# A two-layer hybrid DiT kernel: block 0's rows loaded among the first modulation tiles, and residual-row stores tied to program order

## The chip, the core and the metric

The kernel runs on one core of a Trainium2 chip. The metric is the device time of one execution in microseconds (us). Five engines work side by side: TensorE (PE, matrix multiplies), VectorE (DVE), ScalarE (ACT), GpSimd (POOL) and SyncE (SP). In this kernel SP issues every transfer between HBM and the on-chip memory, in order, on one hardware queue. Each engine works through its own list of instructions in order; when the instruction at its head waits, all that stands behind it on that engine waits too.

## The reference

Two layers, each with a mixer and a feed-forward part, on 1024 latent tokens and 256 context tokens of width 1024:

```python
h = x + _pos_embed_2d(rows, D)[None]
hc = ctx
for l in range(DEPTH):
    mod_x = (silu(c) @ w_mod[l] + b_mod[l])[:, None, :]
    sh1, sc1, gt1, sh2, sc2, gt2 = split(mod_x, 6)      # and mc for the context from c_ctx
    ux = _modulate(h, norm1_g[l], sh1, sc1) @ w_in[l]   # rmsnorm(h) * (1 + scale) + shift
    uc = _modulate(hc, norm1_g[l], mc[0], mc[1]) @ w_in[l]
    # four column groups of u: bidirectional RWKV-7, pooling, 2-D Fourier, gated convolution
    h = h + gt1 * _mix_and_project(ux, y_rwkv_x, ...)
    h = h + gt2 * _swiglu(_modulate(h, norm2_g[l], sh2, sc2), ffn_w_in[l], ffn_w_out[l])
    # the same for hc, except in the last layer
return _rmsnorm(h, final_norm_g)
```

## The kernel before, in words

The width of 1024 is held as NK = 8 rows of 128 partitions. The tokens are three blocks: block 0 and block 1 with 512 latent tokens each, block 2 with the 256 context tokens. A tile of the residual stream is `h[k][tb]`, row k of block tb, 128 x 512 or 128 x 256 floats. A matrix product is made of three TensorE products, since weights and activations are each split into a high part (ACT, `split`, L324) and a low part (L325).

**Order of the work.** The program is traced as straight code with Python generators that are woven into one another. A list scheduler then sets the order of the instructions of each engine, from priorities that follow the order of tracing and from a timeline of its own. What it chooses is fixed in the program; at run time every engine follows its list. `s.pin(...)` (L164, `keep_in_program_order`) takes an instruction out of that choice: it is issued behind the instruction of the same engine that was traced just before it.

**The start (`run`, L1256 to L1293).** The modulation vectors of layer 0 come first: scale (j = 1) and shift (j = 0), two halves each, four generators in the list `mods`. Each has eight tiles of `in_wmod` of 256 KB (`mod_tile`, L216). Two generators use TensorE (`mod_pe`), one DVE (`mod_sum` with `dve`, L261 and L263), one ACT and POOL (`mod_sum` without it, L266, L269 and L267). Then `load(0, k)` loads the eight rows of block 0 (L1266) and adds the position rows on DVE (L1275). The sums of squares of block 0 (`norm_r`, `rstd_g`: ACT squares, TensorE sums into `ps`, ACT root, DVE reciprocal L354, TensorE spread into `ps`) give the norm; `norm_g` (L388, L389, L390) writes the normed activations, and `first_tb` multiplies them by the first columns of `in_win` into `pf`. Blocks 1 and 2 follow.

**The projections of a layer.** `start()` (L1309 to L1316) loads the Fourier tiles `swA` and `swB` and stores all rows `h[k][tb]` to HBM as `hd`, because the residual is needed again only at the output projection: 24 stores in layer 0 (16 of 256 KB, 8 of 128 KB), 16 in layer 1. In layer 0 it is called after the first columns have been shifted (`shift`, L400 to L405; one Tanh part, L784) and stored as `rw` (`spill`, L446). Beside it runs `conv1`: each of its column blocks is multiplied into a `pc` bank of PSUM, of which there are two, and ACT copies the bank out (`dense_tb`, L427). Its results go to HBM (`hc`, L446) and come back as shifted windows (`window`, L506) for the 31-tap convolution on DVE, ACT and POOL (L522 to L535). Meanwhile a second set of modulation tiles for layer 0 (`mod_step`) comes through L216 and is taken by ACT (L269 for the first tile, L266 after it) and POOL (L267), and by TensorE.

The loop of TensorE products of one row block (`dense_tb`) and the loop of the stores are short:

```python
s.mm(ps[:, :n], wh, ah, i == 0, False)
s.mm(ps[:, :n], wh, al, False, False)
s.mm(ps[:, :n], wl, ah, False, i == NK - 1)
```

Of the kernel before, what the change touches and what calls it, by code (L numbers as in the profile page):

```python
# [19 lines left out]
NK = 8  # L20
# [72 lines left out]
class _Kernel:  # L93
# [1162 lines left out]
    def run(s, nlayers):  # L1256
        nc = s.nc
        s.consts()

        h = s.rows(NK, ("x", "c"))  # L1260
# [17 lines left out]
        for k in range(NK):  # L1278
            for g in mods:
                next(g)  # L1280
        for k in range(NK):
            load(0, k)
        s.lab("norm1")
        r = [s.norm_r(h, 0, sq="c2")]
# [15 lines left out]
        for l in range(nlayers):  # L1300
# [6 lines left out]
            hd = [s.dr.tile([128, 1280], F32, name=s.nm("hd")) for _ in range(NK)]  # L1307

            def start(h=h):  # L1309
                for i in range(2):  # L1310
                    nc.sync.dma_start(swA[i], s.I["swA"][l][:, i * 512:(i + 1) * 512])
                    nc.sync.dma_start(swB[i], s.I["swB"][l][:, i * 512:(i + 1) * 512])
                for tb in tbs:
                    for k in range(NK):
                        n = TBS[tb][2]
                        nc.sync.dma_start(hd[k][:, 512 * tb:512 * tb + n], h[k][tb])  # L1316

            hid = [s.dr.tile([128, 1280], F32, name=s.nm("hid")) for _ in range(NFF)]
            h2, acts2 = [[None] * 3 for _ in range(NK)], [[None] * 3 for _ in range(NK)]
# [44 lines left out]
            s.weave = _Weave(s, None)  # L1364
            s.weave.start(side())
            s.rwkv1(l, R, first, acts, ("x", "c") if not last else ("x",), segs, swA, ymix, start)
            s.rwkv2(R, fill())
            h, acts = h2, acts2
# [35 lines left out]
            for k in range(NK):  # L1404
                for tb in tbs:
                    n = TBS[tb][2]
# [6 lines left out]
            for f0, f1 in FF2:  # L1413
                s.lab("ffn2")
                hr = [s.act_row(segs) for f in range(f0, f1)]
                for f in range(f0, f1):
                    for tb in tbs:
                        n = TBS[tb][2]
# [291 lines left out]
class _Weave:  # L1710
# [5 lines left out]
    def next(s, g, end):  # L1716
        s.k.lab(s.labs.get(g, s.k.label))
        r = next(g, end)
        s.labs[g] = s.k.label
        if r is end and g in s.tails:  # L1720
            s.tails.remove(g)
        return r
# [169 lines left out]
```

## Time and profile before

| | us |
|---|---|
| median of 3 runs | 3349.17 |
| the three runs | 3340.93, 3349.17, 3352.15 |
| profiled execution | 3351.38 |
| its span, first to last instruction | 3349.6 |

| engine | busy us | share of the span |
|---|---|---|
| PE | 3000.7 | 90% |
| DVE | 2109.8 | 63% |
| POOL | 1385.8 | 41% |
| ACT | 1257.5 | 38% |

The span is 1.8 us shorter than the profiled execution's own time, and that execution is 2.2 us above the median of the runs. A row of an engine's timeline gives the start in us, the duration, the engine, the source line with the operation, what is written from what is read (buffer numbers left out), shapes, a count where several follow each other, and in brackets the idle time before it and what ended it. In a row for several instructions the duration runs from the start of the first to the end of the last. SPq rows are issues of transfers, not the transfers themselves. A table by windows gives for each stretch the busy time and count of PE, PE's weight loads, DVE, ACT and POOL, then the granted TensorE clock as a share of full speed, the busy share of the DMA engines, and GB/s.

### The profile page before, as it was taken

To read this page: it belongs to the slowest core of one execution; us is meant where nothing else is said; L and a number is where in the kernel's file an instruction comes from. 1 tells how busy PE (TensorE), PEld (TensorE's weight loads), DVE (VectorE), ACT (ScalarE), POOL (GpSimd) and SP (SyncE) were. 2 spreads that over 40 slices of the span, in tenths; PEclk is the share of its full clock that TensorE was granted. 3 is DMA by queue.
4 is the path that set the end of the run, shared out by engine and by line. 5 is a ranking of instruction groups with operands and counts; after the bars stand their busy time and mean duration, and the time that the engine had idled before them with its cause. 6 is when DMAs were issued, how large, how long until landed. Compare 5 with 4: busy or idle time off the path is not lost.

```text
span 3349.6 us, 52386 instructions
## 1 busy us (share of the span) xinstructions
PE 3000.7 (90%) x18888; PEld 2410.5 (72%) x18888; DVE 2109.8 (63%) x3498; ACT 1257.5 (38%) x2575; POOL 1385.8 (41%) x1484
## 2 busy tenths in 40 slices
PE   6989997877889999999999978988877799999998
PEld 3657765766678888888888766756665588888787
DVE  6679666666374988644545598666665755554535
ACT  4446433443363222223212455333443433333212
POOL 2366224563168554435310064245550454545400
PEclk8989887787899999999999988987787799999999
DMA  7422344465455444337412212345553322224312
GB/s 265 165 92 97 102 117 136 124 174 156 144 190 164 149 132 151 125 98 233 139 35 78 87 53 90 117 134 139 156 159 88 128 92 79 82 89 164 123 39 78
DMA packets 375818, 415.48 MB, mean 124 GB/s; under 512 B 115587, under 2 KB 214916, under 8 KB 375558
## 3 DMA queue, kind: packets, MB, share of 16 engines
q1 hardware_dynamic: 375558, 412.13, 39.4%
q8 instruction: 149, 2.44, 0.3%
q14 instruction: 111, 0.91, 0.1%
HBM read 306.49 MB, written 100.27 MB: 121 GB/s over the span
## 4 chain that ended last, share of the span: by engine, by line
PE 55%; DVE 14%; DMA 9%; issue 3%; SPq 1%; ACT 1%; POOL 1%; DVEq 0%; POOLq 0%; ACTq 0%
PE pc L153 17%; PE ps L153 17%; PE pb L153 14%; PE pf L153 8%; DMA t<-Ad 3%; DVE c L532 2%; DMA Td<-t 1%; DVE t L1050 1%; DVE t L947 1%; DVE t L1043 1%; DVE f L325 1%; DVE t L956 1%; DVE t L1469 1%; DMA t<-ho 1%; DVE t L1493 1%
## 5 line engine op out<-in xcount | busy, mean ns | idle before, releaser
L153 PE MATMUL pc<-t,f 128*128 128x512 f32 (+1 forms) x3108 | 754.4, 392 | 41.3 <-ACT t L427 16.0
L153 PEld LDWEIGHTS pc<-t,f 128*128 128x128 f32 x3108 | 581.6, 195 | 182.9 <-ACT t L427 20.5
L153 PE MATMUL ps<-t,f 128*128 128x512 f32 (+1 forms) x2094 | 517.0, 393 | 18.4 <-ACT t L324 7.7
L153 PE MATMUL pb<-t,f 128*128 128x512 f32 (+1 forms) x2094 | 470.5, 370 | 8.4 <-ACT t L1468 4.9
L153 PEld LDWEIGHTS ps<-t,f 128*128 128x128 f32 x2094 | 390.8, 190 | 99.8 <-ACT t L324 8.2
L153 PEld LDWEIGHTS pb<-t,f 128*128 128x128 f32 x2094 | 370.4, 190 | 78.8 <-ACT t L1468 6.0
L1515 ACT CAST f<-c 128x512 fp32r<-128x512 f32 x316 | 196.0, 621 | 536.7 <-PE ps L153 132.0
L1517 POOL TENSOR_TENSOR f<-c,f 128x512 fp32r<-128x512 f32 x135 | 186.5, 1381 | 426.2 <-ACT f L1515 411.7
L153 PE MATMUL pf<-t,f 128*128 128x512 f32 (+2 forms) x1500 | 314.2, 364 | 14.2 <-DVE t L1044 4.0
L324 ACT CAST f<-m 128x512 fp32r<-128x512 f32 (+1 forms) x236 | 134.7, 576 | 436.3 <-PE pb L153 226.4
L153 PEld LDWEIGHTS pf<-t,f 128*128 128x128 f32 (+1 forms) x1500 | 249.5, 198 | 61.4 <-ACT f L324 4.4
L530 POOL TENSOR_TENSOR c<-c,cp 128x352 f32<-128x352 f32 (+2 forms) x168 | 183.3, 1092 | 145.9 <-ACT c L523 71.3
L1517 DVE TENSOR_TENSOR f<-c,f 128x512 fp32r<-128x512 f32 x181 | 158.6, 878 | 134.8 <-ACT f L1515 134.4
L153 PE MATMUL pf<-c,f 128*128 128x512 f32 (+1 forms) x704 | 200.5, 416 | 30.0 <-DVE t L1684 20.3
L325 POOL TENSOR_TENSOR t<-c,t 128x512 fp32r<-128x512 f32 (+1 forms) x110 | 135.1, 1266 | 173.8 <-PE ps L153 99.5
L153 PE MATMUL ps<-t,t 64*128 64x128 f32 (+2 forms) x1032 | 159.9, 341 | 38.9 <-DVE t L956 23.4
L532 DVE SCALAR_TENSOR_TENSOR c<-c,dv,c 128x352 f32<-128x352 f32 (+2 forms) x238 | 190.5, 829 | 2.0
L153 PEld LDWEIGHTS ps<-t,t 64*128 64x128 f32 (+1 forms) x1032 | 133.6, 231 | 60.4 <-issue 20.4
L153 PEld LDWEIGHTS pc<-t,t 128*64 128x64 f32 (+2 forms) x2484 | 124.6, 161 | 71.8 <-issue 28.6
L153 PE MATMUL pc<-t,t 128*64 128x64 f32 (+3 forms) x2484 | 156.2, 258 | 20.9 <-DMA t<-t 11.8
L153 PEld LDWEIGHTS pf<-c,f 128*128 128x128 f32 x704 | 131.5, 214 | 60.1 <-issue 19.1
L261 DVE SCALAR_TENSOR_TENSOR cp<-m,sc,cp 128x512 f32<-128x512 f32 x140 | 137.5, 1003 | 43.0 <-DMA m<-in_wmod 42.3
(256 smaller groups left out, 4731.3 us busy)
## 6 DMA issues: line engine op xcount, KB each, us to landing
c<-in_ffin SPq DMA_DIRECT2D x176, 256.0 KB
m<-in_wmod SPq DMA_DIRECT2D x116, 256.0 KB
t<-rw SPq DMA_DIRECT2D x232, 128.0 KB
hid<-t SPq DMA_DIRECT2D x88, 256.0 KB
c<-hid SPq DMA_DIRECT2D x88, 256.0 KB
m<-in_ffout SPq DMA_DIRECT2D x80, 256.0 KB
t<-in_wmod SPq DMA_DIRECT2D x76, 256.0 KB
m<-in_win SPq DMA_DIRECT2D x64, 256.0 KB
```

What stands on the lines that cost most here:

```text
L153: s.nc.tensor.matmul(o, l, r, start=start, stop=stop)
L261: nc.vector.scalar_tensor_tensor(acc[t], w, sc, acc[t], ALU.mult, ALU.add)
L324: r = s.nc.scalar.copy(hi, src)
L325: (eng or s.lo_eng).tensor_tensor(lo, src, hi.bitcast(F32), ALU.subtract)
L530: nc.gpsimd.tensor_tensor(g, g, t_, ALU.add)
L532: nc.vector.scalar_tensor_tensor(a, w[:, j:j + m], tap(j), a, ALU.mult, ALU.add)
L947: nc.vector.scalar_tensor_tensor(KRv[:, :, p, 0, 1:64], k2[:, :, p, 1:64], -2.0, P2[:, :, p, 0:63], ALU.mult, ALU.mult)
L956: nc.vector.tensor_tensor(BKv[rows, :, :, 1 - h, :], cv(kd)[rows], cv(iP)[rows], ALU.mult)
L1043: nc.vector.tensor_tensor(tv, at(x, o, [0, m], [1, 4], [32, 4]), at(T_, r0, [32, m], [0, 4], [1, 4]), ALU.mult)
L1050: nc.vector.tensor_tensor(tv, at(x, o + 4, [0, m], [1, n], [32, 4]), at(T_, r0, [32, m], [0, n], [1, 4]), ALU.mult)
L1515: nc.scalar.copy(hi, x)
L1517: (nc.gpsimd if s.nw % 7 in LOP else nc.vector).tensor_tensor(lo, x, hi.bitcast(F32), ALU.subtract)
```

## The change

The rows of block 0 are loaded (and the position rows added) inside the loop over the first modulation tiles: row k after the k-th tile of each of the four generators, where they had followed all 32 tiles. And each of the `hd` stores of `start()` is pinned to program order.

```diff
         for k in range(NK):
             for g in mods:
                 next(g)
-        for k in range(NK):
             load(0, k)
         s.lab("norm1")
         r = [s.norm_r(h, 0, sq="c2")]
...
                 for tb in tbs:
                     for k in range(NK):
                         n = TBS[tb][2]
-                        nc.sync.dma_start(hd[k][:, 512 * tb:512 * tb + n], h[k][tb])
+                        s.pin(nc.sync.dma_start(hd[k][:, 512 * tb:512 * tb + n], h[k][tb]))
```

The scheduler answers both edits with a new order. Three places of it follow; a name such as `t2_275_994` is one tile, and the same tile has the same name before and after. One line number falls by one behind the first edit, so L1316 becomes L1315.

SP in layer 0, before, where the `rw` stores and the second modulation set begin (the 24 `hd` stores stand much earlier, after the loads of the `x` rows):

```order
L1312 DMA t2_204_846<-in_swB 128x512
L216 DMA t2_275_994<-in_wmod 128x512
L302 DMA m2_363_1439<-in_win 128x512
L302 DMA m2_366_1445<-in_win 128x512
L446 DMA rw251_893<-t2_257_899 128x512
L216 DMA t2_276_1011<-in_wmod 128x512
L446 DMA rw251_893<-t2_258_900 128x512
L446 DMA rw251_893<-t2_259_901 128x256
L446 DMA rw251_893<-t2_260_919 128x512
L216 DMA t2_280_1032<-in_wmod 128x512
L446 DMA rw251_893<-t2_261_920 128x512
L446 DMA rw251_893<-t2_262_921 128x256
```

The same place after; between the first three `hd` rows and the last one shown stand the other 20:

```order
L1311 DMA t2_204_846<-in_swB 128x512
L446 DMA rw251_893<-t2_258_900 128x512
...
L446 DMA rw251_893<-t2_262_921 128x256
L1315 DMA hd221_863<-t2_1_102 128x512
L1315 DMA hd222_864<-t2_3_104 128x512
L1315 DMA hd223_865<-t2_5_106 128x512
...
L1315 DMA hd228_870<-t2_20_121 128x256
L216 DMA t2_275_994<-in_wmod 128x512
L216 DMA t2_276_1011<-in_wmod 128x512
L216 DMA t2_280_1032<-in_wmod 128x512
```

All 24 `hd` stores have moved from the start to a place between the last `rw` store and the first tile of the second modulation set, `t2_275`; that tile was issued ahead of the first `rw` store before.

ACT at the same place, before (`t2_273` and `t2_274` are written from `t2_275`; `t2_269` and `t2_270` are the copies out of the two `pc` banks):

```order
L784 ACTIVATE t2_257_899<-t2_257_899 128x512
L269 ACTIVATE t2_273_992<-t2_275_994,sc_69 128x512
L269 ACTIVATE t2_274_993<-t2_275_994,sc_69 128x512
L427 COPY t2_269_976<-pc_272_979 128x512
L784 ACTIVATE t2_258_900<-t2_258_900 128x512
L784 ACTIVATE t2_259_901<-t2_259_901 128x256
L266 ACTIVATE t2_277_1013<-t2_276_1011,sc_69 128x512
L266 ACTIVATE t2_278_1016<-t2_276_1011,sc_69 128x512
L324 CAST f2_329_1268<-m2_328_1266 128x512
L266 ACTIVATE t2_281_1034<-t2_280_1032,sc_69 128x512
L266 ACTIVATE t2_282_1037<-t2_280_1032,sc_69 128x512
L427 COPY t2_270_977<-pc_279_1019 128x512
```

And after:

```order
L784 ACTIVATE t2_257_899<-t2_257_899 128x512
L784 ACTIVATE t2_258_900<-t2_258_900 128x512
L784 ACTIVATE t2_259_901<-t2_259_901 128x256
L269 ACTIVATE t2_273_992<-t2_275_994,sc_69 128x512
L269 ACTIVATE t2_274_993<-t2_275_994,sc_69 128x512
L427 COPY t2_269_976<-pc_272_979 128x512
L266 ACTIVATE t2_277_1013<-t2_276_1011,sc_69 128x512
L266 ACTIVATE t2_278_1016<-t2_276_1011,sc_69 128x512
L266 ACTIVATE t2_281_1034<-t2_280_1032,sc_69 128x512
L266 ACTIVATE t2_282_1037<-t2_280_1032,sc_69 128x512
L427 COPY t2_270_977<-pc_279_1019 128x512
```

The two copies out of the `pc` banks stand behind the modulation activations in both; what has moved is the rest of the Tanh parts (ahead of L269) and a cast (behind the second copy).

TensorE at the start, before (`ps_84_338` is the spread of the norm factor of block 0 that L388 reads, `pf_108_403` one of the four last sums of the modulation, `t2_29` and `t2_30` its two halves):

```order
L153 MATMUL ps_74_286<-c2_82_329,cv_73 32x128 x4
L153 MATMUL pf_108_403<-cv_73,t2_29_138 128x1
L153 MATMUL pf_108_403<-cv_73,t2_30_139 128x1
L153 MATMUL pf_108_403<-cv_73,t2_29_138 128x1
L153 MATMUL pf_108_403<-cv_73,t2_30_139 128x1
L153 MATMUL ps_84_338<-c2_83_335,cv_73 128x128 x4
```

And after:

```order
L153 MATMUL pf_105_383<-cv_73,t2_25_129 128x1
L153 MATMUL pf_107_397<-cv_73,t2_106_395 128x2 x4
L153 MATMUL ps_84_338<-c2_83_335,cv_73 128x128 x4
L153 MATMUL pf_108_403<-cv_73,t2_29_138 128x1
L153 MATMUL pf_108_403<-cv_73,t2_30_139 128x1
```

The spread of the norm factor now stands ahead of the last modulation sums, where it stood behind them. In the start SP's list has one row of block 0 after each four modulation tiles, the `hd` stores are gone from it, and the `in_win` loads of `conv1` have come up ahead of the rows of block 1; DVE's list has one L1275 between each pair of L261. In layer 1 the 16 `hd` stores, of which all stood ahead of `swA`, now stand behind it: 6 ahead of the first `rw` store, 10 among the `rw` stores and up to the first `hc` store. In the RWKV stretches of both layers (about 540 to 1050 us and 2160 to 2640 us) rows of SP, PE and DVE change places too, by up to some 110 places.

## Rows read from the trace of the kernel before

**Rows 1.** The profile's page, busy time of each engine over the span.

```profile
PE 3000.7 (90%) x18888; PEld 2410.5 (72%) x18888; DVE 2109.8 (63%) x3498; ACT 1257.5 (38%) x2575; POOL 1385.8 (41%) x1484
```

**Rows 2.** Table by windows (PE, PEld, DVE, ACT, POOL, clock, DMA share, GB/s).

```profile
120.80:124.10 3.30, 3.14 (x7) 2.49 (x8) 1.57 (x1) 2.89 (x6) 3.30 (x3) 0.50 0.37 130
124.20:200.00 75.80, 75.80 (x330) 50.63 (x329) 49.96 (x59) 36.67 (x67) 47.36 (x38) 0.95 0.49 167
200.00:340.00 140.00, 116.74 (x582) 88.37 (x580) 137.10 (x207) 81.31 (x160) 88.03 (x91) 0.89 0.27 88
```

**Rows 3.** Timeline of PE, 0 to 200 us.

```profile
53.13 1.87 PE L153 MATMUL pf<-cv,t 128*128 128x1 f32 x8
...
59.02 0.79 PE L153 MATMUL pf<-t,f 128*128 128x512 f32 x1 [2.10 <-DVE c L388]
...
104.69 13.94 PE L153 MATMUL pc<-t,f 128*128 128x512 f32 x72
120.96 14.44 PE L153 MATMUL pc<-t,f 128*128 128x512 f32 x63 [2.34 <-ACT t L427]
```

**Rows 4.** Timeline of SP's issues, 0 to 170 us.

```profile
47.43 14.88 SPq L1316 DMA_DIRECT2D hd<-t  x23
...
105.89 0.43 SPq L216 DMA_DIRECT2D t<-in_wmod  x1
...
111.82 0.43 SPq L216 DMA_DIRECT2D t<-in_wmod  x1
...
115.78 0.44 SPq L216 DMA_DIRECT2D t<-in_wmod  x1
116.31 0.88 SPq L446 DMA_DIRECT2D rw<-t  x2
```

**Rows 5.** Timeline of ACT, 100 to 215 us.

```profile
110.79 0.63 ACT L784 ACTIVATE t<-t 128x512 f32<-128x512 f32 x1
112.06 1.34 ACT L269 ACTIVATE t<-t,sc 128x512 f32<-128x512 f32 x2 [0.64 <-DMA t<-in_wmod]
113.30 0.57 ACT L427 COPY t<-pc 128x512 f32<-128x512 f32 x1
...
115.23 1.34 ACT L266 ACTIVATE t<-t,sc 128x512 f32<-128x512 f32 x2 [0.53 <-DMA t<-in_wmod]
...
119.11 1.33 ACT L266 ACTIVATE t<-t,sc 128x512 f32<-128x512 f32 x2 [1.38 <-DMA t<-in_wmod]
120.35 0.56 ACT L427 COPY t<-pc 128x512 f32<-128x512 f32 x1
```

**Rows 6.** Timeline of DVE, 0 to 125 us.

```profile
50.36 3.09 DVE L1275 TENSOR_TENSOR t<-t,t 128x512 f32<-128x512 f32 x5
...
56.95 4.04 DVE L388 SCALAR_TENSOR_TENSOR c<-t,A,ps 128x512 f32<-128x512 f32 x6 [1.72 <-PE ps L153]
...
114.22 0.21 DVE L404 SCALAR_TENSOR_TENSOR t<-t,pv,t 128x1 f32<-128x1 f32 x1
```

**Rows 7.** Timeline of PE, 195 to 245 us.

```profile
207.46 1.86 PE L153 MATMUL pf<-t,sc 128*2 128x512 f32 x2 [3.26 <-DMA t<-in_wmod]
...
231.17 1.87 PE L153 MATMUL pf<-t,sc 128*2 128x512 f32 x2 [4.96 <-DMA t<-in_wmod]
```

**Rows 8.** Table by windows in layer 1, columns as in the first such table.

```profile
1860.00:1880.00 20.00, 20.00 (x96) 16.32 (x98) 8.34 (x13) 5.34 (x10) 0.11 (x1) 1.00 0.31 105
...
1960.00:1980.00 20.00, 11.18 (x48) 8.94 (x48) 20.00 (x24) 9.27 (x18) 12.84 (x12) 0.85 0.07 25
```

**Rows 9.** Timeline of SP's issues in layer 1, 1840 to 1930 us.

```profile
1917.01 0.41 SPq L446 DMA_DIRECT2D rw<-t  x1
...
1922.03 0.32 SPq L506 DMA_DIRECT2D c<-hc  x1
```

**Rows 10.** Timeline of DVE in layer 1, 1900 to 1960 us.

```profile
1924.49 0.46 DVE L522 TENSOR_SCALAR c<-c,dv,pv 128x352 f32<-128x352 f32 x1 [1.55 <-DMA c<-hc]
```

**Rows 11.** The chain that ended last, in the RWKV stretch of layer 1.

```profile
2354.92 11.06 DMA t<-Ad
```

## The prediction

> **What bounds the kernel now.** I read the page first, then the table by windows, then the timelines of the places that the new order touches. TensorE is busy for 90% of the span [rows 1], so an edit on the transfers can win only where TensorE waits, and it loses in full wherever it makes TensorE wait and nothing later has room. The windows tell where there is room [rows 2]: from 124.2 to 200 us TensorE is busy all 75.80 us; from 200 to 340 us it is busy 116.74 of 140, but there DVE is busy 137.10. So a delay at 120 us meets first a full TensorE and then a full DVE. The timelines of TensorE, ACT and SP around 104 to 121 us are what the change turns over. TensorE runs 72 products in a row from 104.69, three accumulations of 24, then stands 2.34 us for an ACT copy of L427 [rows 3]. With two `pc` banks, the third accumulation needs the first copy, the fourth needs the second. On ACT the first copy (113.30) stands behind the L269 pair, which waited for a modulation tile until 112.06, and the second (120.35) behind an L266 pair that waited for a tile until 119.11 [rows 5]. Already in the kernel before, then, TensorE is held here through ACT by the modulation tiles on SP.
>
> **The start (0 to 104.7 us): -1 us.** The 24 stores leave SP's list and the rows of block 0 come up among the tiles. The adds of L1275 stay 8, the modulation products on DVE stay the same, so DVE has the same sum to do before the norm. What moves is the norm's factor: TensorE spreads it ahead of the last eight modulation sums (1.87 us) and not behind them [rows 3], and the reciprocal has fewer adds of other rows ahead of it (a group of five took 3.09 us, 0.62 each, at 50.36 [rows 6]). L388 waited 1.72 us for that spread, until 56.95 [rows 6], and TensorE's first product waited 2.10 us for L388, until 59.02 [rows 3]. The best that can come of it is those 2.10 us and the 1.87 us, -4. But the eight sums are still ahead of the first product on TensorE, only 1.87 us of work lies there in place of the wait, and the rows of block 1 now load behind the `in_win` tiles, so that their adds fall among L388 and L390: eight adds of 0.62 us are +5 at worst. From there to 104.69 TensorE is the longer engine. I take -1, nearer the row of the 2.10 us: they look gained, and half may be given back, and keep -4 to +5.
>
> **The second modulation set behind 24 stores: +18 us.** This is the term that decides. Before, tile `t2_275` is issued at 105.89, ahead of the `rw` stores; the 0.64 us that ACT waited for it cost little [rows 4, 5]. After, SP issues it behind all six `rw` stores and all 24 `hd` stores. The last `rw` store needs L404 on DVE, done at 114.22 + 0.21 = 114.43 [rows 6]; the last two `rw` stores at 0.44 us each (0.88 for two [rows 4]) put the end of their issue at about 115.4. For the 24 stores the nearest row is that of 23 of the same stores at the start: 14.88 us [rows 4], 0.65 each, with transfers of other tiles in flight. Eight of the 24 are half size. At 0.45 us per issue (0.43 to 0.44 in the rows of single issues) they take at least 10.8 us; at the row's pace 15.5. I take 13.5, between the two, as the queue is nearly empty of other loads then. So `t2_275` is issued at 115.4 + 13.5 = 128.9 (126.2 to 130.9).
>
> From issue to use a tile took 115.23 - 111.82 = 3.41 us and 119.11 - 115.78 = 3.33 us [rows 4, 5]; behind the stores I take 3.4: ACT starts the L269 pair at 132.3 (129.6 to 134.3), where it had been 112.06. The pair and the copy then take the same time as before, from 112.06 to 113.30 + 0.57 = 113.87, 1.81 us: the first copy ends at 134.1. By then TensorE has long done the two accumulations that have a bank, 48 of its 72 products: 104.69 + 13.94 x 48/72 = 114.0, or 115 if the start is late in its own feed. It stands 19.1 to 20.1 us, taken as 19.6; before it stood 2.34 [rows 3], so 17.3 us are new. The second copy costs nothing on top: ACT has four more L266 ahead of it (two pairs of 1.33 us, their tiles issued right behind `t2_275`) and ends it at 134.1 + 2.66 + 0.56 = 137.3, while TensorE has the third accumulation to do from 134.1, 24 products or 4.65 us. The clock was at 0.50, its 1.2 GHz level, for the 3.3 us behind the wait of 2.34 us [rows 2]; that was paid before too, so I add only +0.5 us for a longer wait. The sum is 17.8, taken as **+18**. The bounds are +11 (stores at the 10.8 us of issue, which is -2.7, and a few us absorbed in DVE's 25.8 idle us of 124.2 to 200) and +21 (the row's pace of the stores, +2, and a longer half clock).
>
> A page of the Trainium skill gives a price for one transfer: "DMA: Bandwidth & Descriptors", section "Anatomy of one DMA — SWDGE (gpsimd) path", about 2.0 us plus the bytes over 436 GB/s, an estimate of 2.6 us for a 256 KB tile. The rows have 3.3 to 3.4, on another path, and I keep the rows; by the page the sum would be 0.8 us less. The Trainium skill's "Perfetto Trace Analysis", section "DMA Optimizations", also says that it may make sense to give loads and stores an issuing engine each. That speaks against what the new order does, 24 stores ahead of a load on one queue; without them in between, `t2_275` would go out at about 115.4 and the term would be some 4 us (115.4 + 3.4 + 1.81 = 120.6 for the first copy, against 114.0 and the old 2.34), the sum +5. No run so far shows stores on an engine other than SP.
>
> **Layer 1: +2 us.** The 16 stores free the `in_win` loads ahead of `swA`, but TensorE is full there (20.00 of 20.00 at 1860 us [rows 8]), so nothing is won. Ten stores now stand between the first `rw` store and the window of the first convolution, at 0.45 us 4.5 us; the last `rw` store was issued at 1917.01 and the window at 1922.03 [rows 9], and DVE's first L522 waited 1.55 us for it, until 1924.49 [rows 10]. DVE then becomes the bound (20.00 of 20.00 at 1960 us [rows 8]), so a late window is in part a late end. Bounds 0 and +4.5; I take +2, about the middle.
>
> **RWKV stretches: 0 us.** The rows that change places there are the same work. The trace has no row for the new order; the nearest price is one wait of the chain on a stored and reloaded tile, 11.06 us [rows 11]. One such wait more or one less gives -11 to +11, kept in the range at ten.
>
> Sum: -1 + 18 + 2 + 0 = +19. The profiled execution took 3351.38 us (its span of 3349.6 and 1.8 around it), so one like it would take 3370.4; the median lies 2.2 lower, so I predict **3368 us**. A measurement of this kernel tells about 0.3%, 10 us, from no change.
>
> **The rivals.** *DVE's idle time takes the wait, and the new order wins elsewhere (faster).* Place: 124.2 to 340 us. DVE has 75.80 - 49.96 = 25.8 us idle in the first stretch [rows 2]. If its convolution work there is not fed by the late TensorE, the 18 us go into that idle time and the end of the stretch at 340 us stands where it was. Then the start (-4 at best) and one RWKV wait of 11.06 us less are left: 3349 - 4 - 11 = 3334, and it counts as faster from -10 us. The point from which it decides is whether the convolution's windows leave TensorE's delayed `pc` stream by more than 16 us. For: DVE's idle time is real. Against: TensorE has none there, and conv1's columns, which the windows read, are products of that very stream. Chance 0.11.
>
> *Half of it is absorbed (same).* Beyond 200 us TensorE waits 3.26 and 4.96 us for modulation tiles [rows 7]. Those are loaded on SP, which is not held by TensorE, and would be there in time if TensorE comes 18 us late: 8 us come back, and with the +11 end of the stall the sum is -1 + 11 - 8 + 2 = +4, 3353 us. Against: DVE is nearly full in that stretch, and it, not TensorE, sets its end. Chance 0.20.
>
> *The new order of the RWKV stretches adds to it (slower by more).* One wait of the 11.06 us kind more: 3379 us, and with the +21 end 3382. Chance 0.14.
>
> *The change does not do what it says.* The stores could also be issued where they stood; but the new list has them behind the `rw` stores, and a list is kept, so this has next to no chance.
>
> **How the numbers follow.** My own case, +19 with its terms near the values above, has 0.55, the slower rival 0.14, the same 0.20, the faster 0.11. Slower by over 0.3% is 0.55 + 0.14 = 0.69, same 0.20, faster 0.11. The likeliest case's own range goes from -4 + 11 + 0 = +7 to -1 + 21 + 4.5 = +24.5, 3356 to 3374 from the median. The range of 8 in 10 takes in the slower rival to its end and a little over, 3386, and the same rival with its lower part, 3343: it leaves out the faster rival but for its edge, and the far ends of the others.
>
> **What the profile will show.** Right: SP's list with 24 stores at about 115 to 129 us; ACT's L269 with an idle time of some 18 to 20 us before it, ended by `in_wmod`; a PE row of 48 `pc` products from about 104, then an idle time of 17 to 20 us ended by ACT's L427; DVE late by the same in 200 to 340 us; L388's first row near 54 and the first product of `first_tb` between 57 and 59. Wrong: an L269 that waits under 8 us; a PE stream that is 16 us late at 130 us and not late at 340; layer 1 shifted by over 5 us against the end of layer 0; or RWKV stretches whose length differs by over 10 us from before.

## The result, and the profile after

The changed kernel took a median of 3392.04 us (3387.85, 3389.67, 3394.41, 3399.60) against 3350.66 for the kernel before on the same chip: ratio 1.0143, 95% interval 1.0121 to 1.0164. That is 1.43%, or 48 us (41 to 55), slower, where 3368 was forecast (19 us above the table's median) and 3386 was the upper end. The two medians by themselves lie 41 us apart; the ratio is used throughout. In the experiments below "+n us" is always the ratio's excess times 3350 us, taken against runs of the kernel before beside it, since that kernel's own medians lie between 3337 and 3351. Medians are of all executions, while the ratios leave out the five single ones that took over 4100 us.

The page after, busy time of each engine over a span of 3386.1 us:

```profile
PE 2995.6 (88%) x18888; PEld 2403.8 (71%) x18888; DVE 2106.6 (62%) x3498; ACT 1261.5 (37%) x2577; POOL 1393.3 (41%) x1484
```

TensorE is busy 5 us less than in [rows 1] and the span is 36.5 us longer: the loss is waiting, not work. To see where it arises, take each instruction's start after minus its start before (median over the instructions that start in a stretch of the trace of before):

| stretch of before, us | shift, us |
|---|---|
| 60 to 110 | -0.9 |
| 110 to 200 | +19.9 |
| 400 to 500 | +22.2 |
| 1100 to 1300 | +37.3 |
| 1600 to 1800 | +38.7 |
| 2100 to 2150 | +31.9 |
| 2700 to 2900 | +46.2 |
| 3150 to 3300 | +35.9 |

So there are three losses and a gain: 20 us at 110 us, 15 in layer 0's RWKV stretch, then 7 back at the start of layer 1, and 14 more in layer 1's RWKV stretch. The last fall, from 46.2 to 35.9, is no gain of the change but one instruction of the profiled execution before, shown at the end; without it the change costs 46 us in the traces as well, in line with the 48. A step of this table is good to some 5 us only: stretches in one and the same order differ by up to 10 us between two executions (the table by groups below).

The stall at 110 us, after. SP's issues, TensorE and ACT, one fence each:

```profile
112.11 2.87 SPq L446 DMA_DIRECT2D rw<-t  x5
115.03 15.29 SPq L1315 DMA_DIRECT2D hd<-t  x24
130.43 2.31 SPq L216 DMA_DIRECT2D t<-in_wmod  x5
```

```profile
103.79 11.07 PE L153 MATMUL pc<-t,f 128*128 128x512 f32 x48
135.27 17.75 PE L153 MATMUL pc<-t,f 128*128 128x256 f32 x85 [20.41 <-ACT t L427]
```

```profile
133.41 1.33 ACT L269 ACTIVATE t<-t,sc 128x512 f32<-128x512 f32 x2 [21.22 <-DMA t<-in_wmod]
134.65 0.56 ACT L427 COPY t<-pc 128x512 f32<-128x512 f32 x1
```

Read them from the bottom: the copy that frees TensorE's bank stands behind L269, L269 waits 21.22 us for the first modulation tile, and that tile is issued only when 24 stores are through. TensorE does the 48 products that have a bank and stands 20.41 us, where [rows 3] had 2.34. Table by windows after, columns as in [rows 2]:

```profile
115.00:135.20 20.20, 0.00 (x0) 0.00 (x0) 0.00 (x0) 1.79 (x4) 0.00 (x0) 0.62 0.97 354
135.20:215.00 79.80, 77.83 (x338) 52.59 (x339) 47.05 (x57) 39.67 (x72) 47.69 (x39) 0.93 0.45 154
215.00:360.00 145.00, 116.61 (x604) 87.16 (x602) 142.86 (x212) 85.13 (x167) 96.19 (x95) 0.94 0.28 91
```

In the stall no compute engine but ACT works, and the DMA engines are busy for 0.97 of it at 354 GB/s: the stores went at the pace of the transfers, not of the issue. Then TensorE and DVE are as full as in [rows 2] (DVE 142.86 of 145), so nothing is made up.

### The profile page after: what moved, and what is told of

Read it like the earlier page. It is cut to its first block, busy times and chain, and to the rows that moved or that the text cites. A ratio compares the mean times of both kernels' runs of the same rounds, so it can differ in the third digit from the quotient of the medians.

```text
span 3386.1 us, 52336 instructions
## 1 busy us (share of the span) xinstructions
PE 2995.6 (88%) x18888; PEld 2403.8 (71%) x18888; DVE 2106.6 (62%) x3498; ACT 1261.5 (37%) x2577; POOL 1393.3 (41%) x1484
## 4 chain that ended last, share of the span: by engine, by line
PE 60%; DVE 20%; DMA 9%; issue 4%; ACT 2%; SPq 2%; POOL 2%; DVEq 0%; POOLq 0%; ACTq 0%
PE pc L153 18%; PE ps L153 16%; PE pb L153 14%; PE pf L153 11%; DVE c L532 4%; DMA t<-Ad 2%; DVE t L1050 1%; DVE t L956 1%; DMA Td<-t 1%; DVE t L1043 1%; DVE t L1052 1%; DVE g L1051 1%; DVE t L401 1%; DVE t L261 1%; DVE t L402 1%
## 5 line engine op out<-in xcount | busy, mean ns | idle before, releaser
L325 POOL TENSOR_TENSOR t<-c,t 128x512 fp32r<-128x512 f32 (+1 forms) x110 | 138.0, 1294 | 162.0 <-PE ps L153 83.3
L153 PE MATMUL ps<-t,t 64*128 64x128 f32 (+2 forms) x1032 | 160.7, 339 | 45.1 <-DVE t L991 21.8
L261 DVE SCALAR_TENSOR_TENSOR cp<-m,sc,cp 128x512 f32<-128x512 f32 x140 | 137.8, 1005 | 46.9 <-DMA m<-in_wmod 46.1
```

What stands on the lines that cost most here:

```text
L153: s.nc.tensor.matmul(o, l, r, start=start, stop=stop)
L261: nc.vector.scalar_tensor_tensor(acc[t], w, sc, acc[t], ALU.mult, ALU.add)
L325: (eng or s.lo_eng).tensor_tensor(lo, src, hi.bitcast(F32), ALU.subtract)
```

## The experiments

In the diffs below, "order" is the list of instructions that an engine works through, one to a row. For all runs but the first two the program was written out with a list of its own: behind the kernel, an order edge from each instruction of an engine to the next holds the engine to it. No run has the list of before written out unchanged, so the cost of these edges by themselves was not measured; the run that moves two rows of it and nothing else (`m1_two_scans_ahead`) bounds it, +2 us (-2 to 7).

```diff
-        K.run(nlayers)
+        K.run(nlayers); _replay(tc)
+def _replay(tc):
...
+            if last is not None:
+                tc.add_manual_dep(i, last, info, reason="order")
+            last = i.name
```

**Each edit alone.** `e1_loads_only` has the loads among the tiles and no pins, `e2_pins_only` the pins and the loads where they were.

```diff
# e1_loads_only
-        for k in range(NK):
             load(0, k)
# e2_pins_only
-                        nc.sync.dma_start(hd[k][:, 512 * tb:512 * tb + n], h[k][tb])
+                        s.pin(nc.sync.dma_start(hd[k][:, 512 * tb:512 * tb + n], h[k][tb]))
```

> Only the first edit: block 0's rows load among the first modulation tiles, the stores are not pinned; they stay ahead of the rw stores, and the tile t2_275 goes out ahead of them as before. Theory (two causes: a stall of about 20 us behind the 24 stores of layer 0, and a new order of the RWKV stretches that costs some 15 us in layer 0 and some 8 us in layer 1): no stall, ACT's L269 waits under 3 us, the start is 0 to 2 us shorter; the RWKV stretches have an order of their own again, which may cost anything between before's and the changed kernel's, so 3340 to 3372 us. Rival (the RWKV stretches are longer only because the stall makes everything come late; their order does not matter): no stall, so no loss, within 5 us of before, 3345 to 3356 us.

> Only the second edit: the stores pinned, block 0's rows loaded after all 32 tiles as before. Theory: the stall of layer 0 is there in full (L269 waits 19 to 22 us), +20, and the RWKV stretches have an order of their own, +0 to +25 more: 3368 to 3395 us. Rival (late feed alone): the same loss as the changed kernel, 3387 to 3397 us.

Loads alone: 3362.42, ratio 1.0071 [1.0052, 1.0090], +24 us; pins alone: 3385.65, 1.0140 [1.0123, 1.0156], +47. The loads bring no stall (shift 1.8 us at 110 to 200 us, 5.7 at 500 to 540), and yet the shift is 17.0 at 1100 us. The pins bring the stall (19 us), and go from 21.8 to 29.9 and from 25 to 48.4 us in the two RWKV stretches. So either edit reorders the RWKV stretches, each in its own way: the loads lose in layer 0's (the 4 us more in layer 1's tell nothing), the pins in both. The two losses do not add up: together they cost what the pins cost alone.

**The start apart from the rest.** `h1_start_of_after` has the order of after for what starts before 540 us and the order of before behind it, `h2_rest_of_after` the reverse.

```diff
# h1_start_of_after: order of SP, one place
-L216 DMA t2_275_994<-in_wmod 128x512
 L446 DMA rw251_893<-t2_262_921 128x256
+L1315 DMA hd221_863<-t2_1_102 128x512
...
+L216 DMA t2_275_994<-in_wmod 128x512
# h2_rest_of_after: these rows as before; from 540 us on as after
```

> No scheduling choice left: each engine's order is written out. Instructions that started before 540 us in the kernel before stand in the order of the changed kernel (its interleaved start and its 24 stores ahead of t2_275), all others in the order of the kernel before, both layers' RWKV stretches and layer 1's stores among them. Theory: the stall of layer 0 alone, +20 us, 3366 to 3375 us, and the shift against before stays about 20 us from 300 us to the end. Rival (late feed alone): the whole loss is there, 3387 to 3397 us.

> The reverse: instructions that started before 540 us in the kernel before stand in its own order, all others in the order of the changed kernel. Theory: no stall at 115 us, the new order of the rest costs +23 to +27 us, 3372 to 3380 us. Rival (late feed alone): nothing is late, so within 5 us of before, 3345 to 3356 us.

The start: 3368.04, 1.0085 [1.0069, 1.0102], +28, over the +20 expected; its shift is 20.0 us at 110 us, 23.7 at 400 and 21.1 at 2700. The rest: 3363.60, 1.0066 [1.0048, 1.0085], +22. 28 and 22 make 50, against 48 for the change: the two halves add up, and nearly half of the loss is not in the start.

**The stores' place.** `h3_stores_early` is the first of these two with the 24 stores moved ahead on SP, right behind the last `x` row; `h4_after_stores_early` is the change with the same move.

```diff
# h3_stores_early, h4_after_stores_early: order of SP
 L1266 DMA t_20_121<-in_xT 128x256 x2
+L1315 DMA hd_863<-t_1_102 128x512
...
+L1315 DMA hd_870<-t_20_121 128x256
 L302 DMA m_328_1266<-in_win 128x512
...
 L446 DMA rw_893<-t_262_921 128x256
-L1315 DMA hd_863<-t_1_102 128x512
...
-L1315 DMA hd_870<-t_20_121 128x256
 L216 DMA t_275_994<-in_wmod 128x512
```

> As the run with the changed kernel's order up to 540 us and the order of before behind it, but SP issues the 24 layer 0 stores right behind the last x row, where the queue has nothing to do until 102 us. Theory (the place of the stores is the whole of the stall): the first tile of the second modulation set goes out behind the last rw store alone, at about 115.4 us, ACT's L269 waits 5 to 7 us and not 21, TensorE some 6 us and not 20; 14 to 17 us shorter than the run with the stores behind the rw stores, +2 to +9 us against before. Rival (the delay comes from the interleaved start or from the tile's own lateness, the stores are beside it): still over +17 us against before.

> The changed kernel's order everywhere, only the 24 layer 0 stores issued right behind the last x row. Theory: the stall goes (14 to 17 us), the cost of the new order of the RWKV stretches stays: +24 to +34 us against before. Rival (late feed alone): with the stall gone the rest goes too, within 6 us of before.

3358.84, 1.0039 [1.0024, 1.0055], +13, over the +9 expected; and 3376.00, 1.0107 [1.0084, 1.0131], +36, over the +34. The move is worth 15 us in the one and 12 in the other, known to some 8 and 11 us; the shift at 110 to 200 us falls by 15.5 and 14.7. SP, ACT and TensorE of `h3_stores_early`:

```profile
57.11 15.40 SPq L1315 DMA_DIRECT2D hd<-t  x24
114.31 2.74 SPq L216 DMA_DIRECT2D t<-in_wmod  x5
```

```profile
119.33 1.33 ACT L269 ACTIVATE t<-t,sc 128x512 f32<-128x512 f32 x2 [7.54 <-DMA t<-in_wmod]
```

```profile
121.18 17.13 PE L153 MATMUL pc<-t,f 128*128 128x256 f32 x85 [6.74 <-ACT t L427]
```

The same stores take 15.40 us there as well, and TensorE's wait falls from 20.41 to 6.74. What is left is the tile behind the `rw` stores. So two thirds of the stall are the stores' place, not their number. The other 13 us of the start's +28 are that remnant (shift 4.5 us at 110 us, 8.8 at 540) and a few us that no run tells apart.

**The later stretches, one by one.** The order of before, but that of after for what starts in 540 to 1060 us (`h5_rwkv0_only`), 2160 to 2660 us (`h6_rwkv1_only`), 1840 to 2160 us (`m2_layer1_start`). `Ad` and `Td` are tiles in HBM: a solve reads its matrix back from `Ad`, and its result goes out to `Td` and comes back.

```diff
# h5_rwkv0_only: order of DVE, one place
+L926 SCALAR_TENSOR_TENSOR t_682_3063<-t_592_2604,t_663_2960 128x512
 L354 RECIPROCAL t_811_3892<-t_811_3892 128x128
 L1031 TENSOR_TENSOR g_5333<-t_721_3288 128x4x2
...
-L926 SCALAR_TENSOR_TENSOR t_682_3063<-t_592_2604,t_663_2960 128x512
# h6_rwkv1_only: order of SP, one place
+L1056 DMA Td_21274<-t_3775_20164 4x256x32
...
 L1001 DMA t_3662_19537<-Ad_21190 128x1x512
 L1001 DMA t_3663_19538<-Ad_21190 128x1x512
-L1056 DMA Td_21274<-t_3775_20164 4x256x32
# m2_layer1_start: order of SP, one place (9 of 16 stores move)
-L1316 DMA hd_17791<-t_2673_14631 128x512
 L1311 DMA t_3291_17764<-in_swA 128x512
...
+L1316 DMA hd_17791<-t_2673_14631 128x512
 L446 DMA rw_17814<-t_3349_17822 128x256
```

> The order of before everywhere, except that the instructions that started between 540 and 1060 us in it (the RWKV stretch of layer 0) stand in the changed kernel's order. Theory (order of this stretch): +7 to +15 us against before, all of it made between 600 and 1050 us. Rival (what is fed late): within 4 us of before.

> The order of before everywhere, except that the instructions that started between 2160 and 2660 us in it (the RWKV stretch of layer 1) stand in the changed kernel's order. Theory (order of this stretch): +12 to +18 us against before, made between 2250 and 2600 us. Rival (what is fed late): within 4 us of before.

> The order of before, except that the instructions that started between 1840 and 2160 us in it (layer 1's projections and convolution, with its 16 pinned stores) stand in the changed kernel's order. Theory (read from the shift between the two traces, which falls from 43 us at 2000 to 32 us at 2150): 4 to 8 us shorter than before; the window of the first convolution is 4 to 7 us late and this is more than made up. What I predicted for this stretch: +2 us.

| run | median, us | ratio, interval | us |
|---|---|---|---|
| `h5_rwkv0_only` | 3356.95 | 1.0045 [1.0029, 1.0062] | +15 |
| `h6_rwkv1_only` | 3351.93 | 1.0035 [1.0021, 1.0049] | +12 |
| `m2_layer1_start` | 3334.23 | 0.9979 [0.9967, 0.9991] | -7 |

15 + 12 - 7 = 20, against the +22 of the rest; with the start's 28 the parts make 48, and the change measured 48. By the intervals of the four parts that sum is good to some 10 us. The order of the two RWKV stretches, the same work throughout, costs 27 us.

The traces of all runs bear this out. The table gives what the shift gains over a stretch (taken between the stretches of the first table: 400 to 500, 1100 to 1300, 1600 to 1800, 2100 to 2150 and 2700 to 2900 us), in each trace with the order of before there and in each with that of after:

| stretch | order of before, us | order of after, us |
|---|---|---|
| layer 0's RWKV | -7.8 to +1.9 (9 traces) | +7.6 to +15.1 (4) |
| layer 1's start | -1.8 to +0.3 (12) | -6.8 to -5.6 (5) |
| layer 1's RWKV | -0.3 to +9.9 (6) | +13.8 to +19.3 (5) |

In no stretch do the two groups overlap, but within a group one trace differs from another by up to 10 us.

**What in layer 0's RWKV stretch.** DVE after and, second, before, at the first solves (L1031 starts a solve on a stored and reloaded `Ad`; L926 is a scan that waits for POOL's L921):

```profile
619.17 1.62 DVE L926 TENSOR_TENSOR_SCAN t<-t,t 128x512 f32<-128x512 f32 x1 [13.08 <-POOL t L921]
621.56 0.36 DVE L1031 TENSOR_TENSOR g<-t 128x8 f32<-128x8 f32 x1
...
656.37 1.62 DVE L926 TENSOR_TENSOR_SCAN t<-t,t 128x512 f32<-128x512 f32 x1 [10.00 <-POOL t L921]
667.03 1.10 DVE L1031 TENSOR_TENSOR g<-t 128x8 f32<-128x8 f32 x1
```

```profile
598.22 1.62 DVE L926 TENSOR_TENSOR_SCAN t<-t,t 128x512 f32<-128x512 f32 x1 [2.82 <-POOL t L921]
...
634.09 0.17 DVE L1031 TENSOR_TENSOR g<-t 128x8 f32<-128x8 f32 x1 [3.46 <-DMA t<-Ad]
```

After, the scan stands ahead of the solve and waits 13.08 and 10.00 us with the solve behind it; before, it stood behind and waited 2.82. That looks like the loss. `n1_two_solves` takes after's order for these two solves alone (584 to 672 us, all engines), `m1_two_scans_ahead` moves only the two scans, and `m3_scans_later` does the opposite to the order of before: six scans that waited go behind rows of the solve that were ready.

```diff
# m1_two_scans_ahead: order of DVE, whole difference
+L926 SCALAR_TENSOR_TENSOR t_682_3063<-t_592_2604,t_663_2960 128x512
 L354 RECIPROCAL t_811_3892<-t_811_3892 128x128
...
-L926 SCALAR_TENSOR_TENSOR t_682_3063<-t_592_2604,t_663_2960 128x512
...
+L926 SCALAR_TENSOR_TENSOR t_682_3063<-t_592_2604,t_663_2960 128x512
 L1031 TENSOR_TENSOR g_5810<-t_721_3288 128x4x2
...
-L926 SCALAR_TENSOR_TENSOR t_682_3063<-t_592_2604,t_663_2960 128x512
# n1_two_solves: these two rows, and the other rows of 584 to 672 us
# m3_scans_later: order of DVE, one of six places
+L1052 TENSOR_TENSOR t_749_3454<-t_749_3454,g_5333 128x2x24
+L1043 TENSOR_TENSOR t_749_3454<-t_721_3288,t_749_3454 128x48
...
 L926 SCALAR_TENSOR_TENSOR t_682_3063<-t_592_2604,t_663_2960 128x512
-L1052 TENSOR_TENSOR t_749_3454<-t_749_3454,g_5333 128x2x24
```

> The order of before, except that the instructions of all engines that started between 584 and 672 us in it (two triangular solves of layer 0 and the preparations beside them) stand in the changed kernel's order. Theory (the loss of layer 0 is made where the solves' lag behind the reload grows, 9 and 6 us to 17 and 20 us): +5 to +10 us, there by 720 us. Rival (spread over the whole stretch): 0 to +4 us.

> The order of before with two rows of DVE moved, nothing else: in the RWKV stretch of layer 0 the scan L926 of two preparations stands ahead of the reciprocal L354 and the first row L1031 of the triangular solve, as in the changed kernel, and not in the middle of the solve. The scan waits for POOL's L921, and the solve behind it with it. Theory (the cost of the new order is DVE rows that wait in front of the solve): the two solves start 5 to 10 us later against the reload of their tiles, +5 to +14 us at the end. Rival (the order of DVE there is not what costs; the reloads on SP or POOL's rows are): the solve's delay is made up before 700 us, within 3 us of before.

> The reverse of the two moved scans: the order of before, and on DVE the rows of the solve that are ready stand ahead of six scans L926 that waited 2.3 to 6.3 us for POOL's L921 with those rows behind them (four in layer 0, two in layer 1; 52 rows moved). Theory (the solve is the chain, what stands in front of it on DVE is paid): each solve ends 2 to 4 us sooner, 5 to 15 us shorter in all. Rival: the preparation of the next solve comes as much later as this one ends sooner, within 4 us of before.

Two solves: 3353.95, 1.0034 [1.0018, 1.0049], +11 (6 to 16), where the whole stretch has +15 (10 to 21). Two scans: 3344.78, 1.0007 [0.9994, 1.0021], +2, with the long waits in place:

```profile
598.60 1.62 DVE L926 TENSOR_TENSOR_SCAN t<-t,t 128x512 f32<-128x512 f32 x1 [13.36 <-POOL t L921]
...
642.53 1.22 DVE L926 TENSOR_TENSOR_SCAN t<-t,t 128x512 f32<-128x512 f32 x1 [8.07 <-POOL t L921]
```

The solves did start 17.64 and 11.69 us behind the issue of their reload (9.42 and 5.95 before), but the shift at 700 us was 3. The rival was right: the long wait before L926 is made up within the solve and costs 7 us at most. Scans later: 3335.16, 0.9988 [0.9975, 1.0001], -4, just short of the -5 expected and of being told from nothing.

So by its time `n1_two_solves` has most of the loss, but its trace does not show it there, where it was expected "by 720 us". The shift rises from -6.0 at 580 to 600 us to +4.7 at 620 to 640, is back at -3.4 by 700 to 720 and stays there; over the whole stretch it gains -3.8, which lies within the group of before's order. The four traces with the whole stretch in after's order rise again by 6.5 to 9.7 us from 680 to 700 us to 720 to 740, behind this run's window. (The traced execution, 3347.63, is the third fastest of its twelve.) That the order of layer 0's RWKV stretch costs 15 us is shown; in which rows is open.

**What in layer 1's RWKV stretch.** Here SP's list looked guilty: in the new order the reloads of `Ad` stand behind the store and the reloads of `Td`. Four runs mend the order of `h6_rwkv1_only` at that one solve, step by step.

```diff
# n2_stores_ahead: order of SP
+L995 DMA Ad_21190<-t_3735_19993 32x4x32 x2
+L995 DMA Ad_21190<-t_3737_19995 32x4x32 x2
 L1056 DMA Td_21274<-t_3775_20164 4x256x32
...
-L995 DMA Ad_21190<-t_3735_19993 32x4x32 x2
-L995 DMA Ad_21190<-t_3737_19995 32x4x32 x2
# n3_stores_and_pool: n2, and order of POOL
+L921 TENSOR_SCALAR t_3609_19247<-t_3609_19247 128x512
+L921 TENSOR_SCALAR t_3610_19248<-t_3610_19248 128x512
 L325 TENSOR_TENSOR cp_20748<-t_3870_20745,c_3871_20747 128x512
...
-L921 TENSOR_SCALAR t_3609_19247<-t_3609_19247 128x512
-L921 TENSOR_SCALAR t_3610_19248<-t_3610_19248 128x512
# o1_reload_ahead: n2, and order of SP
+L1001 DMA t_3662_19537<-Ad_21190 128x1x512
+L1001 DMA t_3663_19538<-Ad_21190 128x1x512
 L1056 DMA Td_21274<-t_3775_20164 4x256x32
...
-L1001 DMA t_3662_19537<-Ad_21190 128x1x512
-L1001 DMA t_3663_19538<-Ad_21190 128x1x512
# o2_rwkv1_again: h6_rwkv1_only unchanged
# p1_reload_and_pool: o1, and order of POOL
-L1018 TENSOR_SCALAR t_3775_20164<-cv 128x256
...
 L1035 TENSOR_TENSOR t_3663_19538<-t_3663_19538,g_21399 128x4x2
+L1018 TENSOR_SCALAR t_3775_20164<-cv 128x256
```

> The RWKV stretch of layer 1 in the changed kernel's order, all else in the order of before, as in the run that was 12 us longer; but on SP the second four stores L995 of one solve, which stood behind the store L1056 and three reloads L1062 that wait for it (2310.05 us, 9.6 us after the first four), go back to right behind the first four. Theory (SP's in-order wait): the next solve starts 5 to 7 us sooner, +4 to +9 us against before in place of +12. Rival (the solve waits for DVE or POOL anyway): still +10 to +14 us.

> As that, and on POOL the pair L921 of the same solve goes back ahead of two L325 splits of the output projection and one row of the solve. Theory: 2 to 4 us more, so +1 to +6 us against before. Rival: no further gain, as the run with the stores alone.

> The order of before, but layer 1's RWKV stretch (2160 to 2660 us) in the order of after, with one repair on SP, in the one solve where the reload of Ad stood last: the second half's stores of Ad (four L995 rows) and both reloads of Ad (L1001) moved ahead of the store of Td (L1056), the other instructions unchanged. Theory: what this stretch loses is the reload that waits in SP's list behind the store of Td and four reloads of Td; in the run with the stores alone moved, the reload was still issued 8.3 us behind the last store of Ad, where before it was 1.2 us. With the reload moved too it is issued within 2 us of the last store, the solve starts 6 to 8 us sooner, the distance from this solve to the one ahead of it falls from 51 us to 43 to 45 us (before 40.8), and the time is +1 to +6 us against before where the unrepaired stretch is +9 to +14. Rival: the solve starts sooner, but DVE and TensorE give it back in the rest of the stretch, since the chain there is bound by other rows: +9 to +14, no better than the unrepaired stretch beside it.

> The same program without the repair (layer 1's RWKV stretch in the order of after, all else as before), on the same chip beside the repaired one. Both theories: +9 to +14 us against before. The difference of the two programs is 5 to 10 us by the theory of the late reload, under 3 us by its rival.

> The run with the repaired reload, and one row more moved, on POOL in the same solve: L1018, which must wait for the store of Td and stood ahead of POOL's half of the solve (L1029 to L1035), now stands right behind it, about as in the order of before. Theory: two lists, SP's and POOL's, each put the Td work ahead of the solve of Ad, so mending one only moves the wait to the other (there DVE began the solve 8.8 us sooner and then waited 10.05 us for POOL's L1029, which stood behind an L1018 that had waited 19.15 us). With both mended, POOL's L1029 starts within about 3 us of DVE's L1031, the 10.05 us wait of DVE's first L1043 falls under 3 us, the scan L926 behind the solve starts 5 to 8 us sooner against the solve ahead of it, and the time is +2 to +7 us against before, 4 to 8 us under the run with the reload alone (+11). Rival: the 10.05 us are covered, for TensorE and the rest of DVE's list in this stretch are bound by other rows, or the loss goes on to a third list: +9 to +14 again.

| run | median, us | ratio, interval | us |
|---|---|---|---|
| `n2_stores_ahead` | 3352.07 | 1.0026 [1.0013, 1.0039] | +9 |
| `n3_stores_and_pool` | 3355.20 | 1.0037 [1.0022, 1.0051] | +12 |
| `o1_reload_ahead` | 3356.41 | 1.0031 [1.0015, 1.0046] | +10 |
| `o2_rwkv1_again` (not mended) | 3353.37 | 1.0027 [1.0014, 1.0040] | +9 |
| `p1_reload_and_pool` | 3360.74 | 1.0044 [1.0025, 1.0062] | +15 |

No repair gains. Why is to be read in two of the traces. With the reload ahead (`o1_reload_ahead`; SP, then POOL, then DVE):

```profile
2307.17 1.17 SPq L1001 DMA_DIRECT2D t<-Ad  x2
2308.38 0.54 SPq L1056 DMA_DIRECT2D Td<-t  x1
2308.97 8.19 SPq L302 DMA_DIRECT2D m<-in_wout  x1
```

```profile
2319.27 0.41 POOL L1018 TENSOR_SCALAR t<-cv 128x256 f32<-128x256 f32 x1 [19.15 <-DMA Td<-t]
```

```profile
2313.64 0.17 DVE L1031 TENSOR_TENSOR g<-t 128x8 f32<-128x8 f32 x1 [4.92 <-DMA t<-Ad]
...
2324.68 0.19 DVE L1043 TENSOR_TENSOR t<-t,t 128x16 f32<-128x16 f32 x1 [10.05 <-POOL t L1029]
```

The distance from the solve ahead to this one is 45.5 us (2313.64 - 2268.12, where the solve ahead starts; unmended, in `o2_rwkv1_again`, 50.9 with a wait of 11.35 us for `Ad`; before 40.8). But five instructions on DVE waits 10.05 us for POOL, whose half of the solve stands behind an L1018 that waits for the store of `Td`. With L1018 moved as well (`p1_reload_and_pool`; SP, ACT, POOL, DVE):

```profile
2318.77 7.72 SPq L302 DMA_DIRECT2D m<-in_wout  x1
```

```profile
2329.29 0.62 ACT L324 CAST f<-m 128x512 fp32r<-128x512 f32 x1 [12.16 <-DMA m<-in_wout]
```

```profile
2330.04 1.26 POOL L325 TENSOR_TENSOR f<-m,f 128x512 fp32r<-128x512 f32 x1 [20.45 <-ACT f L324]
```

```profile
2334.06 0.19 DVE L1043 TENSOR_TENSOR t<-t,t 128x16 f32<-128x16 f32 x1 [10.31 <-POOL t L1029]
```

DVE waits the same 10.31 us, now by way of a weight tile: its load stands behind the store of `Td` on SP, ACT's cast waits for it, and POOL's L325, which also stands ahead of POOL's half, waits for the cast. The wait did not go; it changed its releaser twice. The repair also moved a long issue on SP. The issue right behind the store of `Td` was a load of `hd` before; unmended, in `o2_rwkv1_again`, it was a weight tile but a short issue. Before, then `o2_rwkv1_again`:

```profile
2312.28 0.54 SPq L1056 DMA_DIRECT2D Td<-t  x1
2312.87 7.70 SPq L1676 DMA_DIRECT2D t<-hd  x1
```

```profile
2305.46 0.57 SPq L1056 DMA_DIRECT2D Td<-t  x1
2306.13 2.23 SPq L302 DMA_DIRECT2D m<-in_wout  x1
```

With the reload ahead the 8 us fall on the weight tile that ACT and POOL wait for, so the two last repairs took one wait away and brought another. My theory of the late reload has fallen as a cause that one row mends. What is shown is that SP's and POOL's lists both put the `Td` group and the weights ahead of this solve. The solve may also be the wrong place: in all nine traces with after's order or a mended one, the shift rises by 4.2 to 6.2 us from 2270 to 2290 us, ahead of the rows that were mended (-0.6 to +2.1 in the six with before's order), and no repair touched that. Whether all the rows mended give the 12 us back was not tried and stays open.

**The two together.** `m4_layer1_and_scans` is the kernel before with the order of after at layer 1's start and with the six scans later.

```diff
# m4_layer1_and_scans: the rows of m2_layer1_start and of m3_scans_later
```

> Both: layer 1's start in the changed kernel's order and the solve ahead of the six waiting scans. Theory: the sum of the two, 9 to 20 us shorter than before. Rival: no better than the better of the two alone.

3328.89 against 3340.86, 0.9961 [0.9946, 0.9976], -13 (-18 to -8): faster than both kernels. That the scans add to layer 1's start, -7 (-11 to -3) alone, is likely but not told apart: the intervals overlap.

## Why the prediction was wrong, by its own steps

- **The stall, +18, was right in mechanism, place and nearly in size.** Forecast were `t2_275` at 128.9, L269 at 132.3 and a wait of 19.6 us; measured 130.43, 133.41 and 20.41. The stores took 15.29 us where I took 13.5 "as the queue is nearly empty of other loads"; the DMA share of 0.97 says what that left out: 24 stores fill the DMA engines by themselves, and the row of 23 stores [rows 4] was the better price. From issue to use it was 133.41 - 130.43 = 2.98 us, under the 3.3 to 3.4 of the rows of before. By the ratio the whole start costs +28 [23 to 34], by the traces 20 to 24; the forecast was 17. What the ratio has above the traces is open. The Trainium skill's "DMA: Bandwidth & Descriptors", section "Anatomy of one DMA — SWDGE (gpsimd) path", gave an estimate of 2.6 us for such a tile on another path; the 2.98 measured here lie above it.
- **The separate engine for stores.** The Trainium skill's "Perfetto Trace Analysis", section "DMA Optimizations", says that it may make sense to give loads and stores an issuing engine each. No run here shows that; moving the stores 58 us ahead on the same queue (115.03 to 57.11) gave 12 to 15 us.
- **The start, -1, was right.** The shift at 60 us is -0.9; the first product came at 55.96 (59.02 in [rows 3]), sooner than the 57 to 59 forecast, but the second at 61.27 (61.28 before), so nothing of it was kept. TensorE, then DVE:

```profile
55.96 0.77 PE L153 MATMUL pf<-t,f 128*128 128x512 f32 x1
...
61.27 0.79 PE L153 MATMUL pf<-t,f 128*128 128x512 f32 x1
```

```profile
52.94 4.04 DVE L388 SCALAR_TENSOR_TENSOR c<-t,A,ps 128x512 f32<-128x512 f32 x6 [1.23 <-PE ps L153]
```

- **"RWKV stretches: 0 us. The rows that change places there are the same work" is the step that failed.** It was +15 and +12. Of the 48 us the forecast lacks 29: these 27 and 11 at the start, less 9 in layer 1. Same work is no argument where lists of five engines and one DMA queue wait for one another: I had listed up to 110 places of moved rows, and priced a wait of 11.06 us [rows 11] as a chance of 0.14 for one such wait, when each of two stretches lost a little more than that. The slower rival, "one wait of the 11.06 us kind more", named the right place and, for one stretch, about the right size. Its mechanism is not shown: with the late reload of `Ad` mended (`o1_reload_ahead`) the loss stayed, so that its size fits is luck as far as the runs tell.
- **"Layer 1: +2 us" had the wrong sign, -7.** The window of the first convolution was issued late as priced, 1964.94 - 1922.03 = 42.9 us against a shift of 38.7 ahead of the layer, +4.2 where 4.5 was the bound. Its first L522 was later still, 1970.38 - 1924.49 = 45.9 us, for on DVE it stands behind an L325 that waited 6.32 us for ACT. But what followed came sooner, down to 31.9 at 2100 us. I followed the stores to the first wait that they lengthen and not to the end of the stretch. SP and DVE after, where [rows 9, 10] stood:

```profile
1958.89 2.40 SPq L1315 DMA_DIRECT2D hd<-t  x4
...
1964.94 0.37 SPq L506 DMA_DIRECT2D c<-hc  x1
```

```profile
1969.77 0.69 DVE L325 TENSOR_TENSOR f<-m,f 128x512 fp32r<-128x512 f32 x1 [6.32 <-ACT f L324]
1970.38 0.46 DVE L522 TENSOR_SCALAR c<-c,dv,pv 128x352 f32<-128x352 f32 x1
```

- **The rivals that absorbed the stall fell.** The shift stays at 20 to 22 us from 110 to 500 us; the modulation tiles that would have been in time by then gave nothing, since DVE is full there.

## What to carry to other kernels

When a scheduler answers an edit with a new order, price the stretches that only moved as well: replay each stretch's order alone, and the parts add up (28 + 15 - 7 + 12 = 48 here, to some 10 us). A long wait in front of an instruction is not its price: two scans moved so that they waited 13 and 8 us cost 2 us, and mending one list only handed the wait to the next. One trace of each kernel is not enough to place a loss of 5 us, as the same order varied by up to 10 us a stretch. Stores whose data is needed late still take their time on the queue, 15 us here for 24, so look at which load stands behind them.

## What was not expected of the hardware

One vector instruction can take 11 us for once. In the profiled execution before, DVE shows this row among others of L325 that take 0.67 and 0.68 us with the same shape; the second fence is POOL at that time:

```profile
3100.18 11.20 DVE L325 TENSOR_TENSOR f<-m,f 128x512 fp32r<-128x512 f32 x1 [3.54 <-ACT f L324]
...
3111.96 0.68 DVE L325 TENSOR_TENSOR f<-m,f 128x512 fp32r<-128x512 f32 x1
```

```profile
3094.68 16.15 POOL L325 TENSOR_TENSOR t<-c,t 128x512 fp32r<-128x512 f32 x13
```

It makes the whole fall of the shift from 46.2 to 35.9 us. The trace of `h5_rwkv0_only` has it too, in the very same row of the list:

```profile
3117.19 11.59 DVE L325 TENSOR_TENSOR f<-m,f 128x512 fp32r<-128x512 f32 x1 [3.22 <-ACT f L324]
```

The other 18 traces have no such row, that of the changed kernel among them; the same row takes 1.71 us in `m2_layer1_start`. In both long cases it ends half a us after a run of POOL's L325 without a gap ends (3110.83 us before). That it waits until POOL pauses fits this, but no run shows it. In any case a difference of 10 us between two traces has to be traced to its row before it is explained.

And an issue on SP can itself be long: the L302 behind the store of `Td` shows 8.19 and 7.72 us in the two traces above, where half of all L302 issues take under 0.4. It is the place and not the load: in the twenty traces 46 issues took over 3 us, up to 8.4, and every one of them stands right behind a store of `Td`. Most of the 400 such stores have no long issue behind them, and what makes the difference is open.
